# Feed-forward seam of a two-layer decoder trunk: earlier weight loads, sums of squares at other products

## The chip, the cores and the metric

The kernel runs on one core of a Trainium2 chip. The metric is the device time of one execution in microseconds (us). The core has a matrix engine (TensorE, "PE" in the profile), three elementwise engines (VectorE "DVE", ScalarE "ACT", GpSimd "POOL") and a queue engine (SyncE, "SP") that issues nearly all DMA transfers. Each engine executes its own instructions in order, and they wait for each other through semaphores.

## The reference, cut to what matters

A trunk of two layers on one sequence of 1024 tokens with 1024 channels. Layer 0 mixes tokens with a gated recurrent block, layer 1 with attention; each mixer is followed by a SwiGLU feed-forward block of width 2816, and each block is preceded by an RMS norm and added to the residual.

```python
def swiglu_ffn(x, w_in, w_out):
    gu = jnp.einsum("bsd,df->bsf", x, w_in)
    h = jax.nn.silu(gu[..., :D_FF]) * gu[..., D_FF:]
    return jnp.einsum("bsf,fd->bsd", h, w_out)
...
for layer in range(DEPTH):
    hn = rms_norm(h, mix_norm[layer])
    if mixer == 0:
        mixed = rg_lru_block(hn, ..., lru_w_in[j], ..., lru_w_out[j], ...)
    else:
        mixed = stick_breaking_attention(hn, attn_w_qkv[j], attn_w_o[j])
    h = h + mixed
    h = h + swiglu_ffn(rms_norm(h, ffn_norm[layer]), ffn_w_in[layer], ffn_w_out[layer])
return rms_norm(h, final_norm)
```

## The kernel before

**Precision.** Every float32 operand of a matrix product is split into a high and a low part, and a product is three matmuls: high by high, high by low, low by high (`mm3`, lines 155 to 157). In the feed-forward input the parts are float16. So the weights are first scaled by a power of two, taken from a bound on their size: the sum of the squares of all the elements.

**The feed-forward input.** It runs in 22 steps, f = 0 to 21; a step computes 128 gate and 128 up columns for all 1024 tokens. A step is done by a seven-product scheme in the manner of Strassen and Winograd: the weights of a step arrive as two tiles, `ra` (gate columns) and `rb` (up columns), VectorE forms sums and differences of their halves (`s12`, `s2`, `s3`, `do_s4`), and seven products of 12 matmuls each go to PSUM, in the order `ORDER` = 0, 1, 2, 3, 4, 6, 5. Below, "product k" is the k-th of a step, from 0. Steps 4 to 19 work in pairs (`PAIRS` holds the even ones); one product of each pair's two steps is replaced by smaller ones (`inner_part`), for which the weights of both steps are needed together (`inner_sums`).

What happens to the weights of a step:

- `weights_in(f)` loads `ra` and `rb` (512 KB each). Up to f = 4 tiles come from a ring of three raw tiles (`load_raw`, line 128), shared with other weights; a load waits until its tile is free. `rb` of f = 3 and 4 goes to two spare tiles of half the size (`loose`, a ring of 11). From f = 5 on a pool of its own serves.
- `Measure` bounds their size: `square` sums the squares of a tile on ScalarE (line 821; two instructions when the tile comes as two halves), `total` adds up the sums on VectorE (line 919), `factors` adds over partitions with a one-column matmul (`over_partitions`, line 251) and derives the power of two with four small VectorE instructions (`power`, lines 244 to 248). Steps of a pair are measured together.
- `a_hi`, `b_hi`, `c_hi`, `d_hi` write the scaled high parts on ScalarE (line 828), `a_lo` to `d_lo` the low parts on VectorE (line 831). Products 0 and 1 use `wa`, products 2 and 4 `wb`, 3 and 6 `wc`, and product 5 `wd`. `wa` is written during the step before, `wb` (`b_lo`) at the start of its own step, `wc` and `wd` within it. Hence the weights of step f+1 (`nw` in the code) must be measured before `nw.a_hi`, while those of step f+2 (`ahead`) are loaded and squared.

**The engines' order.** The feed-forward runs inside `manual_schedule` for PE, ACT, DVE and POOL: the order of instructions on each of them is the order of the program. The queue engine's is left to the framework's scheduler. In the recurrent stage of layer 0 only PE is ordered by hand.

**The seam.** The output projection of the mixer (16 products, o = 0 to 15 in the code) gives the new residual `h`; its float16 parts for the seven products are written by `v_steps` and `v_last`. Step 0's weights are prepared between these products. Step 0 runs its first six products over three quarters of the contraction (54 matmuls), then over the last quarter (18 matmuls, loop over `k` at line 1210), then the seventh product into half 0 of the PSUM tile `ob`. The power of f = 1 is taken through half 1 of the same tile (`m1.factors(half(ob, 1))`). Step 1, with `s_ == 0` in the code, also holds the sums of squares of the residual (`squares`, `stats_mm`, line 1241) and the norm factors (`factors`, line 1253). `late` marks the steps in which `nw.a_hi` and `nw.a_lo` come at products 4 and 5 (steps 1 and 20); elsewhere they come at 2 and 4.

**Planned jobs.** `measure(x, k, nw, ahead)` is called at product k of step x. It enters `square`, `total` and `factors` of a measurement in `plan` under the pair (step, product) at which they are to be issued, and issues those that are due. In layer 0 it also loads parts of the attention's output weights and takes their maxima (`weigh`, line 627, two per step for eight steps), for a bound that layer 1 needs. After the jobs, at the same product, come the gate's instructions (`gate`: a product with the norm factors, Silu on ScalarE, two more products on VectorE) and the operands of the feed-forward's second half (`operands`).

**The recurrent stage.** In layer 0's mixer the stages of `order` (line 582; A and B project, G computes gates, Y multiplies) are issued one after another. Among them `stage_n(i)` loads one of eight row blocks of `lru_w_out` into a raw tile and sums its squares on ScalarE (line 561).

## Time and profile before

| | |
|---|---|
| median of 3 runs | 2109.04 us (2107.64 to 2115.51) |
| profiled execution, its own time | 2109.0 us |
| its span, first to last instruction | 2106.7 us |
| mean granted PE clock | 0.996 |
| recurrent stage with its projections | about 10 to 250 us |
| layer 0, output projection and feed-forward input | about 250 to 740 us |
| layer 1, the same | about 1400 to 1880 us |

The time runs from launch to end; the span is what the profile covers. In a row of a timeline the columns are: start in us, duration in us, engine, source line, operation, tile written and tiles read, shape, count, and in brackets the time that the engine sat idle before the instruction with what ended it. A row of the waits gives engine, tile and line that waited, what it waited for, then the total in us, the number of times, and the longest. Matmuls overlap: the distance of two starts says more than a duration.

### The profile page before, as it was taken

The page shows a single profiled execution, that of the slowest core. Times are in us where ns is not written, and L with a number is a line of the kernel's source. Part 1 is how long each engine was busy: PE and PEld are TensorE (multiplying, and loading weights), DVE is VectorE, ACT ScalarE, POOL GpSimd, SP SyncE. Part 2 cuts the span into 40 slices and gives each one's busy share as a digit, 9 for nine tenths or more (in the row PEclk, how much of TensorE's full clock was granted, in tenths as well). Part 3 has the DMA queues.
Part 4 walks back from the last instruction along what each step waited for, and adds up shares of the span by engine and source line. Part 5 has one row for each costly group of instructions (what it writes and reads, how often), then busy time and mean ns, then how long its engine had stood idle before and what let it go on. Part 6 is the DMA issues. An engine that isn't in the chain of part 4 may idle for free.

```text
span 2106.7 us, 28516 instructions
## 1 busy us (share of the span) xinstructions
PE 2066.1 (98%) x10052; PEld 1410.3 (67%) x10052; DVE 1824.9 (87%) x2789; ACT 1309.3 (62%) x2111; POOL 155.0 (7%) x130
## 2 busy tenths in 40 slices
PE   8999999999999999999999999999899999999998
PEld 7878885454445478888777777777445555558887
DVE  7878877889999888796999999977799999888886
ACT  6667545665656555466788877754665656554456
POOL 1222010000000000000011111202000000000002
PEclk9999999999999999999999999999999999999999
DMA  7221441445554646433888998963154555565452
GB/s 252 87 67 56 143 157 55 143 137 180 181 185 145 222 150 203 138 121 98 157 179 180 179 174 177 239 212 100 57 184 137 171 164 178 181 211 168 127 154 90
DMA packets 450543, 323.35 MB, mean 153 GB/s; under 512 B 166616, under 2 KB 362336, under 8 KB 450400
## 3 DMA queue, kind: packets, MB, share of 16 engines
q1 hardware_dynamic: 450240, 321.28, 53.2%
q8 instruction: 78, 1.28, 0.2%
q14 instruction: 65, 0.53, 0.1%
q10 hardware_dynamic: 160, 0.27, 0.0%
HBM read 193.01 MB, written 82.84 MB: 131 GB/s over the span
## 4 chain that ended last, share of the span: by engine, by line
PE 79%; DVE 13%; ACT 5%; DMA 1%; issue 1%; POOL 0%; SPq 0%; DVEq 0%; ACTq 0%; POOLq 0%
PE p_ps L157 14%; PE p_ps L155 14%; PE p_ps L156 14%; PE qk_ps L155 4%; PE qk_ps L157 4%; PE qk_ps L156 4%; PE av_ps L2076 3%; PE ob_ps L155 3%; PE ob_ps L157 3%; PE ob_ps L156 3%; PE a_ps L156 2%; PE a_ps L157 2%; PE a_ps L155 2%; PE z_ps L1964 2%; PE z_ps L1965 1%
## 5 line engine op out<-in xcount | busy, mean ns | idle before, releaser
L157 PE MATMUL p_ps<-v,wb 128*128 128x512 f16 x352 | 134.2, 381 | 6.8 <-DVE wb L831 6.8
L155 PE MATMUL p_ps<-v,wb 128*128 128x512 f16 x352 | 133.9, 380 | 0.6 <-ACT G L1084 0.6
L156 PE MATMUL p_ps<-v,wc 128*128 128x512 f16 x352 | 134.1, 381 | 0.0
L157 PE MATMUL p_ps<-v,wc 128*128 128x512 f16 x352 | 134.1, 381 | 0.0
L156 PE MATMUL p_ps<-v,wb 128*128 128x512 f16 x352 | 134.0, 381 | 0.0
L155 PE MATMUL p_ps<-v,wc 128*128 128x512 f16 x352 | 134.0, 381 | 0.0
L828 ACT ACTIVATE wb<-sb,fac 128x1024 f16<-128x1024 f32 x44 | 50.5, 1148 | 104.5 <-DVE sb L760 104.5
L155 PE MATMUL qk_ps<-rh,whi 128*128 128x512 f32 x264 | 112.9, 428 | 0.0
L2002 ACT ACTIVATE w<-z_ps,rs 128x512 f32<-128x512 f32 (+2 forms) x168 | 96.9, 580 | 15.4 <-PE z_ps L1965 13.0
L2024 ACT CAST wx<-w 128x512 f16<-128x512 f32 (+1 forms) x140 | 80.1, 572 | 38.5 <-DVE w L2009 20.4
L156 PE MATMUL qk_ps<-rl,whi 128*128 128x512 f32 x264 | 103.5, 392 | 0.0
L157 PE MATMUL qk_ps<-rh,wlo 128*128 128x512 f32 x264 | 103.5, 392 | 0.0
L2009 DVE TENSOR_TENSOR_SCAN w<-w,unit 128x128 f32<-128x128 f32 (+1 forms) x112 | 93.5, 835 | 9.5 <-ACT w L2002 8.3
L232 POOL TENSOR_TENSOR acc<-acc,rbc 128x512 f32<-128x512 f32 x30 | 42.6, 1419 | 764.9 <-ACT rbc L231 727.1
L155 PE MATMUL a_ps<-xh,whi 128*128 128x512 f32 x248 | 97.0, 391 | 0.0
L156 PE MATMUL a_ps<-xl,whi 128*128 128x512 f32 x248 | 96.6, 390 | 0.1
L157 PE MATMUL a_ps<-xh,wlo 128*128 128x512 f32 x248 | 96.6, 389 | 0.0
L821 ACT ACTIVATE junk<-raw 128x1024 bf16<-128x1024 f32 x84 | 88.5, 1053 | 6.1 <-DMA raw<-in_ffn_w_in 6.1
L1332 DVE TENSOR_TENSOR rl<-rl,rh 128x512 fp32r<-128x512 f32 x128 | 83.4, 685 | 4.9 <-ACT rh L1331 4.9
L2025 DVE TENSOR_TENSOR wx<-w,wx 128x512 f16<-128x512 f32 (+1 forms) x140 | 87.3, 624 | 0.2 <-ACT wx L2024 0.2
L155 PE MATMUL p_ps<-v,wa 128*128 128x512 f16 x224 | 85.2, 380 | 0.0
L156 PE MATMUL p_ps<-v,wa 128*128 128x512 f16 x224 | 85.0, 380 | 0.0
(490 smaller groups left out, 6415.7 us busy)
## 6 DMA issues: line engine op xcount, KB each, us to landing
raw<-in_ffn_w_in SPq DMA_DIRECT2D x84, 512.0 KB, 4.2
rl<-pd SPq DMA_DIRECT2D x128, 256.0 KB, 3.1
pd<-U SPq DMA_DIRECT2D x90, 256.0 KB, 2.3
raw<-in_ffn_w_out SPq DMA_DIRECT2D x56, 256.0 KB, 3.3
raw<-in_attn_w_qkv SPq DMA_DIRECT2D x24, 512.0 KB, 4.3
raw<-in_lru_w_out SPq DMA_DIRECT2D x16, 512.0 KB, 3.6
h<-hd SPq DMA_DIRECT2D x32, 256.0 KB, 5.5
hd<-h SPq DMA_DIRECT2D x32, 256.0 KB, 2.2
```

What stands on the lines that cost most here:

```text
L155: nc.tensor.matmul(ps, lhsT=wh, rhs=mh, start=first, stop=False, **kw)
L156: nc.tensor.matmul(ps, lhsT=wh, rhs=ml, start=False, stop=False, **kw)
L157: nc.tensor.matmul(ps, lhsT=wl, rhs=mh, start=False, stop=last, **kw)
L232: (eng or nc.gpsimd).tensor_add(acc[n], acc[n], sq)
L821: nc.scalar.activation(v["junk"][:, 0 : t.shape[-1]], t, AF.Square, accum_out=next(at))
L828: nc.scalar.activation(hi, t, AF.Copy, scale=self.up)
L1332: V.tensor_sub(tl, f32(tl), f32(th))
L2002: nc.scalar.activation(F, ps[:, 0:n], AF.Sigmoid, scale=rs[:, j : j + 1])
L2009: nc.vector.tensor_tensor_scan(rev, rev, unit[:, NB - n :][:, ::-1], 0.0, op0=ALU.mult, op1=ALU.add)
L2024: nc.scalar.copy(wx[:, 0:m, 0], F)
L2025: nc.vector.tensor_sub(wx[:, 0:m, 1], F, wx[:, 0:m, 0])
L2076: nc.tensor.matmul(ps[:, c0:c1].rearrange("p (j c) -> p j c", c=P), lhsT=VV[q][:, hx, kb], rhs=t, start=first and i == 0, stop=last and i ...
```

## The change

It has five parts.

1. Spare tiles. `rb` of f = 1 to 4 (before: 3 and 4) is loaded as two halves into spare tiles.
2. Sooner loads. f = 2 is loaded at product 15 of the output projection (before: after step 0), f = 3 at product 0 of step 1 (before: products 1 and 2), f = 4 at product 4 of step 1 (before: products 0 and 1 of step 2).
3. Sums of squares. f = 2 is measured inside step 0: the power of f = 1 is taken before the last 18 matmuls, f = 2's squares and total follow, and its factors come at product 0 of step 1 (before: squares, total and factors at products 0 to 2 of step 1). f = 3's squares come at products 3 and 4 of step 1 instead of 4 and 5. f = 4 and 5 are squared at products 0, 1, 4 and 5 of step 2 (before 3 to 6). For all pairs the total comes at product 6 of the even step and the factors at product 2 of the odd one (before: products 0 and 1 of the odd one), and `nw.a_hi` at product 3 of the odd step instead of 2. Step 1 is no longer `late`.
4. Maxima. `weigh` takes the maximum at product 1 of the next step instead of product 6 of the step of the load.
5. Recurrent stage. Loading and squaring the rows of `lru_w_out` are separate, at other places of `order`, some of them later.

```diff
+        rows_in = {}
+
+        def load_rows_in(i):
+            rows_in[i] = load_raw(lru_w_out[0][i * P : (i + 1) * P, :].rearrange("p (a b) -> p a b", a=1), (1,))
+
         def stage_n(i):
-            raw = load_raw(lru_w_out[0][i * P : (i + 1) * P, :].rearrange("p (a b) -> p a b", a=1), (1,))
+            raw = rows_in.pop(i)
             nc.scalar.activation(raw, raw, AF.Square, accum_out=wsq[0][:, i : i + 1])
...
-                if 4 <= i < 4 + 2 * ND and i % 2:
-                    stage_n((i - 4) // 2)
+                for do, at in ((stage_n, (7, 8, 12, 13, 17, 18, 22, 23)), (load_rows_in, (5, 7, 11, 12, 15, 17, 20, 22))):
+                    if i in at:
+                        do(at.index(i))
...
-                if f in (3, 4) and x:
+                if 0 < f < 5 and x:
                     raw = loose(v), loose(v)
...
                     elif o == 15:
                         m1.square(0)
+                        nxt = weights_in(2)
+                        m2 = Measure(nxt)
...
             for i in ORDER0[:6]:
                 part(P0[i], w, i, rhs_in[i], range(HK - 1))
+            m1.factors(half(ob, 1))
+            m2.square(0)
+            m2.square(1)
+            m2.total()
             for k, i in enumerate(ORDER0[:6]):
                 part(P0[i], w, i, rhs_in[i], (HK - 1,))
...
                 elif k == 4:
-                    m1.factors(half(ob, 1))
                     nw.a_hi()
...
             nw.do_s4()
-            nxt = weights_in(2)
             nw.c_hi()
...
-                    plan.setdefault((6 + i // 2, 6), []).append(lambda: weigh(i, t))
+                    plan.setdefault((7 + i // 2, 1), []).append(lambda: weigh(i, t))
...
-                if k == 0 and x in (1, NF - 2):
+                if (x, k) == (1, 0):
+                    m, at = m2, ((1, 0),)
+                elif (x, k) == (NF - 2, 0):
                     m, at = Measure(nw), ((x, 0), (x, 1), (x, 1), (x, 2))
                 elif (x, k) == (1, 3):
-                    m, at = Measure(ahead), ((1, 4), (1, 5), (1, 6), (2, 0))
+                    m, at = Measure(ahead), ((1, 3), (1, 4), (1, 5), (2, 0))
...
-                elif k == 3 and x + 2 in PAIRS:
+                elif (x, k) == (2, 0):
+                    m, at = Measure(ahead, early[3]), ((2, 0), (2, 1), (2, 4), (2, 5), (2, 6), (3, 2))
+                elif k == 3 and x + 2 in PAIRS and x > 2:
                     m = Measure(ahead, early[x + 1])
-                    at = ((x, 3), (x, 4), (x, 5), (x, 6), (x + 1, 0), (x + 1, 1))
+                    at = ((x, 3), (x, 4), (x, 5), (x, 6), (x, 6), (x + 1, 2))
...
-                late = kind == "f" and x in (1, NF - 2)
+                late = kind == "f" and x == NF - 2
+                soon = kind == "f" and x + 1 in PAIRS
...
-                        if nw and not late:
+                        if nw and not late and not soon:
                             nw.a_hi()
...
                         if k == 3:
+                            if soon:
+                                nw.a_hi()
                             nw.s12()
...
                     if kind == "f" and x == 1:
-                        if k == 1:
-                            ahead.load_a()
-                        elif k == 2:
-                            ahead.load_b()
-                    elif kind == "f" and x + 2 in PAIRS:
                         if k == 0:
                             ahead.load_a()
-                        elif k == 1:
                             ahead.load_b()
+                        elif k == 4:
+                            early[2] = weights_in(4)
+                    elif kind == "f" and x + 2 in PAIRS:
+                        if k == 0 and x > 2:
+                            ahead.load_a()
+                        elif k == 1 and x > 2:
+                            ahead.load_b()
+                        if k == 0:
+                            early[x + 1] = weights_in(x + 3, False)
                         elif k == 2:
-                            early[x + 1] = weights_in(x + 3, False)
                             early[x + 1].load_a()
```

## The prediction

> **What bounds the kernel now.** I read the page first, then the waits of TensorE (PE) longest first, then the timelines of PE, VectorE (DVE) and ScalarE (ACT) around each long wait.

> ```profile
> span 2106.7 us, 28516 instructions
> ...
> PE 2066.1 (98%) x10052; PEld 1410.3 (67%) x10052; DVE 1824.9 (87%) x2789; ACT 1309.3 (62%) x2111; POOL 155.0 (7%) x130
> ```

> PE is busy 2066.1 of the 2106.7 us span, so about 40 us of gaps are all that a change of order can win, plus the slow matmuls behind the gaps.

> ```profile
> PE n_ps L251 <- DVE part L919: 9.5, 8, 2.4
> PE p_ps L157 <- DVE wb L831: 6.8, 6, 1.8
> PE ob L155 <- DVE sums L244: 4.9, 2, 2.5
> ```

> All three longest rows belong to the measuring of weights (sums of squares, L919; their power, L244) and to splitting them (L831). PE's timeline in layer 0, with the wait before an instruction in brackets, places four stalls A to D at the start of the feed-forward:

> ```profile
> 340.16 0.38 PE L156 MATMUL p_ps<-v,wc 128*128 128x512 f16 x1
> 340.38 0.38 PE L157 MATMUL p_ps<-v,wc 128*128 128x512 f16 x1
> ...
> 347.12 0.38 PE L155 MATMUL ob<-v,wd 128*128 128x512 f16 x1 [2.45 <-DVE sums L244]
> ...
> 348.48 0.63 PE L155 MATMUL ob<-v,wd 128*128 128x512 f16 x1
> 348.91 0.63 PE L156 MATMUL ob<-v,wd 128*128 128x512 f16 x1
> ...
> 351.04 0.63 PE L155 MATMUL p_ps<-v,wa 128*128 128x512 f16 x1
> ...
> 361.75 0.16 PE L251 MATMUL n_ps<-part,one 128*128 128x1 bf16 x1 [2.42 <-DVE part L919]
> ...
> 382.97 0.38 PE L155 MATMUL p_ps<-v,wb 128*128 128x512 f16 x1 [0.30 <-ACT G L1084]
> ...
> 385.35 0.39 PE L157 MATMUL p_ps<-v,wb 128*128 128x512 f16 x1 [1.79 <-DVE wb L831]
> ...
> 407.05 0.16 PE L251 MATMUL n_ps<-part,one 128*128 128x1 bf16 x1 [2.13 <-DVE part L919]
> ```

> A is 347.12, B 361.75, C 382.97 and 385.35, D 407.05. Matmuls normally start 0.22 us apart (340.16, 340.38), but 0.43 apart at 348.48: after A, B and C the clock is halved for some 3.4 us, about eight matmuls, 1.7 us more each. After D no matmul is slow. Layer 1 has the same four, with a halved clock after A alone:

> ```profile
> 1487.61 0.38 PE L155 MATMUL ob<-v,wd 128*128 128x512 f16 x1 [2.44 <-DVE sums L244]
> ...
> 1501.62 0.16 PE L251 MATMUL n_ps<-part,one 128*128 128x1 bf16 x1 [1.80 <-DVE part L919]
> ...
> 1523.55 0.39 PE L157 MATMUL p_ps<-v,wb 128*128 128x512 f16 x1 [1.79 <-DVE wb L831]
> ...
> 1543.56 0.16 PE L251 MATMUL n_ps<-part,one 128*128 128x1 bf16 x1 [2.14 <-DVE part L919]
> ```

> [...]

> **The change part by part.**

> *Stall A.* Before, f=1's power waits on DVE behind three evictions, and PE's product into the same `ob` tile waits for it. Now its over-partitions matmul stands ahead of the last 18 matmuls of step 0, with f=2's squares and total behind it. The rows of ACT and DVE that feed it:

> ```profile
> 341.80 1.04 ACT L821 ACTIVATE junk<-raw 128x1024 bf16<-128x1024 f32 x1
> ...
> 342.83 0.57 ACT L1064 COPY G<-p_ps 128x512 f32<-128x512 f32 x1
> ...
> 375.74 0.62 ACT L821 ACTIVATE junk<-spare 128x512 bf16<-128x512 f32 x1
> ...
> 377.22 1.28 ACT L1104 ACT_TABLE_LOAD   x1
> ```
> ```profile
> 342.96 0.16 DVE L919 TENSOR_REDUCE part<-sums 128x1 bf16<-128x2 f32 x1
> ...
> 344.06 0.75 DVE L831 SCALAR_TENSOR_TENSOR wd<-s,fac,wd 128x512 f16<-128x512 f32 x1 [0.94 <-ACT wd L828]
> ```

> The square of f=1's second half starts at 341.80 (the casts ahead of it are not touched) and takes 1.03 us; as two loose halves it takes 1.48 (375.74 to 377.22). So its total comes at 343.3 and the matmul at 343.5, while PE has finished the earlier products at 340.38 + 0.38 = 340.76: a **new wait of 2.75 us**, again with a halved clock, in place of 2.45. f=2's squares (1.03 + 1.48 = 2.5 us) then push ACT's `d_hi` and DVE's `wd` from 344.06 to 347.0. PE is at half speed until 348.2, finishes the 18 at 349.1, the 12 of `ob` at 351.65: 0.6 late against 351.04, less 0.35 by which the old slow phase reached into step 1: **+0.25** in each layer. A moves, it does not go.

> *Stall B.* f=2's weights wait for a buffer, and ACT waits for them:

> ```profile
> 360.36 1.06 ACT L821 ACTIVATE junk<-raw 128x1024 bf16<-128x1024 f32 x1 [2.34 <-DMA raw<-in_ffn_w_in]
> ```

> Now they are loaded at product 15 of the output projection, into a slot that step 0's own splitting has freed and two spare tiles, and measured before step 1. Its power follows step 1's first product and waits for nothing. DVE, 2.5 us later than before after A, is next to be late: the sums of squares of the residual end about 0.4 (layer 1: 0.25) after PE wants them. Layer 0: −2.42 − 1.7 + 0.4 = **−3.7**; layer 1: −1.80 + 0.25 = **−1.55**.

> *Stall C.* Before, f=2 is split late, and f=3's squares stand ahead of the first Silu's table load:

> ```profile
> 379.70 1.22 DVE L1106 TENSOR_TENSOR G<-ob,G 128x1024 f32<-128x1024 f32 x1 [2.30 <-ACT G L1104]
> ...
> 384.02 1.27 DVE L831 SCALAR_TENSOR_TENSOR wb<-sb,fac,wb 128x1024 f16<-128x1024 f32 x1
> ```

> DVE loses 2.30 us there. Loading f=3 at the first product of step 1 and squaring one product sooner lets the table load run beside DVE's gate; I leave DVE 1.2 of the 2.3, the length of the Silu itself. Step 2 then begins at 373.7, 3.6 sooner by A and B. The Silu ends at 374.1, and from there to the end of `wb` DVE needs 5.5 us, as it did before from 379.70 to 384.02 + 1.27: 379.6, where PE asks at 379.3. The third matmul of that product came 2.4 us late, of which 0.2 stays: layer 0, −2.4 − 1.7 + 0.2 = **−3.9**; layer 1, −2.4 + 0.15 = **−2.25**.

> *Stall D.* The total of f=4 and f=5 stood behind step 3's splits on DVE. It moves to the end of step 2, its factors to product 2 of step 3, and f=4 lands in step 1: nothing is left for PE to wait for, and step 3's `wb` comes within 0.1 of its time. **−2.1** and **−2.05**.

> The two seams: 0.25 − 3.7 − 3.9 − 2.1 = −9.45, and 0.25 − 1.55 − 2.25 − 2.05 = −5.6; together **−15.05**.

> *The pairs, steps 4 to 19.* The total moves ahead of `b_lo`, the power from product 1 to product 2 of the odd step, `a_hi` one product on (ACT has room). Layer 1, DVE, with one row of ACT and one of PE:

> ```profile
> 1649.39 0.75 DVE L831 SCALAR_TENSOR_TENSOR wc<-s,fac,wc 128x512 f16<-128x512 f32 x1 [0.79 <-ACT wc L828]
> ...
> 1652.57 0.15 DVE L244 TENSOR_SCALAR sums<-n_ps 128x1 f32<-128x1 f32 x1
> ...
> 1653.01 0.14 DVE L248 TENSOR_SCALAR fac<-sums 128x1 int32<-128x1 int32 x1
> ...
> 1654.97 0.75 DVE L831 SCALAR_TENSOR_TENSOR wd<-s,fac,wd 128x512 f16<-128x512 f32 x1 [0.69 <-ACT wd L828]
> ...
> 1666.67 1.28 DVE L831 SCALAR_TENSOR_TENSOR wb<-sb,fac,wb 128x1024 f16<-128x1024 f32 x1
> ```
> ```profile
> 1647.59 1.06 ACT L821 ACTIVATE junk<-raw 128x1024 bf16<-128x1024 f32 x1
> ```
> ```profile
> 1668.23 0.38 PE L157 MATMUL p_ps<-v,wb 128*128 128x512 f16 x1
> ```

> The total now waits on DVE for the fourth square, 1647.59 + 1.06 = 1648.65, some 1.3 us, with `b_lo`, `c_lo` and PE's products behind it. The 0.79 and 0.69 that DVE waits anyway take that up. The power (1652.57 to 1653.01, 0.5 with what it keeps from starting) leaves the shadow of the 0.69 and comes after `wd`, from where DVE runs nearly without a gap: `wb`, ended at 1667.95, ends 0.4 later (0.1 is made up on the way), against PE's need at 1668.23. **+0.2** a pair, seven pairs in layer 1 and three in layer 0: **+2.0** (bounds 0 and 0.5 a pair).

> *The maxima of layer 0* (two, 1.2 us, in each of eight steps):

> ```profile
> 478.93 0.16 PE L251 MATMUL n_ps<-part,one 128*128 128x1 bf16 x1 [0.25 <-DVE part L919]
> ```
> ```profile
> 497.20 0.39 PE L157 MATMUL p_ps<-v,wb 128*128 128x512 f16 x1 [0.80 <-DVE wb L831]
> ```

> 0.25 + 0.80 come four times, 4.2 us. Moved behind the splits, the maxima no longer stand directly ahead of `wb`, but in these steps DVE has nothing to spare: the total's 1.3 us and the power take what the move frees. I find stalls of 0.55 and three of 1.1, so **−0.35** (bounds −4.2 and +2).

> *The recurrent stage.* Squares and loads of `lru_w_out` move; DVE, ACT and the queue are not ordered by hand there.

> ```profile
> 152.42 0.49 PE L155 MATMUL g_ps<-rh,whi 128*128 128x512 f32 x1 [2.22 <-ACT rh L512]
> 153.68 0.74 PE L156 MATMUL g_ps<-rl,whi 128*128 128x512 f32 x1 [0.77 <-DVE rl L513]
> ```
> ```profile
> 114.13 1.06 ACT L561 ACTIVATE raw<-raw 128x1024 f32<-128x1024 f32 x1 [1.09 <-DMA raw<-in_lru_w_out]
> ```

> PE's only stall here is 2.22 + 0.77 and a halved clock, 4.7 us. The chain of waits that ends in it passes the square at 114.13: 1.09 of waiting and 1.06 of work. Whether another square takes that place the trace cannot say. Bounds −4.7 and +4.7 (such a stall again); I take **−2**, nearest to the 2.15 us of that row.

> Sum: −15.05 + 2.0 − 0.35 − 2 = −15.4. The profiled execution took 2109.0 us (span 2106.7, 2.3 outside it), as good as the median, 2109.04: **2093.6**.

> **The rivals.** *R1, the waits only move at C and D as at A.* DVE is 2.5 us later after A; if it stays late, `wb` stalls PE at steps 2 and 3. For it: DVE is nearly full in step 2. Against: its wait of 2.30, which is slack. Only B is won, and the small terms: 0.5 − 3.7 − 1.55 − 0.35, with the pairs and the recurrent stage cancelling, is −5.1: 2104. *R2, slower.* The total in DVE's queue at the end of each even step: if the waits of 0.79 and 0.69 do not absorb its 1.3 us, each pair loses 1.3 + 0.5 = 1.8; 15 pairs, 27 us, against −17.4 for the rest: 2119. It decides once DVE reaches `wd` later than ACT has it. Against it: 0.79 + 0.69 is more than 1.3. *R3, the weights land no sooner*, the queue or a slot holding f=2 and f=3: B and part of C stay, 2101. *R4, more:* all of the recurrent stall (−2.7 more), all maxima (−3.9) and no loss in the pairs (−2): 2085.

> **How the numbers follow.** Chances: the forecast 0.60, R1 0.17, R4 0.12, R2 0.06, R3 0.05. Where the halved clock falls differs from stall to stall, which alone moves the forecast by 3 us. The range leaves out R2 and the edge of R4: 2085 to 2104. A measurement here tells about 0.5%, 10.5 us, from no change; below 2098.5 lie R4 and most of the forecast: 0.70. Within 0.5%: 0.25. Slower: 0.05.

> **What would show it.** Right: PE waits near 340.8 for `part` L919 in both layers; no wait on a load of `in_ffn_w_in` at ACT in step 1; no n_ps stall at steps 1 and 3; small `wb` stalls at each even step. Wrong: no wait at A's new place (faster than I say), `wb` stalls of over 1 us in layer 1's pairs (R2), or a stall longer than 2.2 us in the recurrent stage.

## The result and the profile after

| | before | after |
|---|---|---|
| median of 5 runs | 2112.62 us (2107.64 to 2115.51) | 2098.30 us (2096.75 to 2098.69) |
| ratio after to before, 95% interval | | 0.9935 [0.9919, 0.9951] |
| profiled execution, its span | 2109.0, 2106.7 us | 2098.69, 2096.1 us |
| mean granted PE clock | 0.996 | 0.997 |

The kernel became 0.65% faster, and the whole interval lies on that side. The profiled executions differ by 10.3 us, the medians by 14.3 us: the profiled execution of before lies near the lower end of its runs.

The page of after, and its longest PE waits (engine, tile and line, what it waited for; total in us, times, longest):

```profile
span 2096.1 us, 28530 instructions
...
PE 2063.3 (98%) x10052; PEld 1410.0 (67%) x10052; DVE 1823.8 (87%) x2789; ACT 1311.3 (63%) x2119; POOL 148.5 (7%) x130
```
```profile
PE ob L251 <- DVE part L925: 5.5, 2, 2.7
PE p_ps L157 <- DVE wb L837: 4.3, 6, 0.9
...
PE g_ps L155 <- ACT rh L512: 2.0, 1, 2.0
PE p_ps L155 <- ACT G L1092: 1.6, 5, 0.5
PE p_ps L157 <- DVE wa L837: 1.5, 1, 1.5
PE n_ps L251 <- DVE part L925: 1.2, 2, 0.9
```

The lines of the file moved: L919 is L925 now, L831 is L837, L821 is L827, L1084 is L1092. The stall of n_ps fell from 9.5 to 1.2 us and that of `wb` from 6.8 to 4.3; the wait for `ob` was 4.9 and is 5.5 in a new place. PE's timeline shows the places, first layer 0's seam and step 20, then layer 1's seam:

```profile
344.79 0.16 PE L251 MATMUL ob<-part,one 128*128 128x1 bf16 x1 [2.74 <-DVE part L925]
...
353.42 0.39 PE L157 MATMUL p_ps<-v,wa 128*128 128x512 f16 x1 [1.48 <-DVE wa L837]
...
358.88 0.38 PE L155 MATMUL p_ps<-v,wb 128*128 128x512 f16 x1 [0.52 <-ACT G L1092]
...
381.58 0.39 PE L157 MATMUL p_ps<-v,wb 128*128 128x512 f16 x1 [0.47 <-DVE wb L837]
...
712.29 0.16 PE L251 MATMUL n_ps<-part,one 128*128 128x1 bf16 x1 [0.87 <-DVE part L925]
...
1476.98 0.16 PE L251 MATMUL ob<-part,one 128*128 128x1 bf16 x1 [2.74 <-DVE part L925]
1477.01 0.38 PE L155 MATMUL p_ps<-v,wa 128*128 128x512 f16 x1
...
1478.46 0.63 PE L156 MATMUL p_ps<-v,wa 128*128 128x512 f16 x1
1478.88 0.63 PE L157 MATMUL p_ps<-v,wa 128*128 128x512 f16 x1
```

Stall A is still there (2.74 us at the over-partitions matmul, once in each layer). B and D are gone; of C 0.47 us is left. New are 1.48 us for `wa` in layer 0, 0.52 us for `G` behind it, and 0.87 us at step 20.

To see where time went I took PE's matmuls of both traces in their order and subtracted the start times. The line between A and B is drawn behind the wait for `wa`, ahead of the one for `G`. What each stretch adds, after minus before, beside the forecast:

| stretch | forecast, us | measured, us |
|---|---|---|
| up to step 0 of layer 0 (recurrent stage) | −2 | +1.3 |
| layer 0: A and B | 0.25 − 3.7 = −3.45 | +0.3 − 3.6 = −3.3 |
| layer 0: C | −3.9 | −3.5 |
| layer 0: D | −2.1 | −2.3 |
| layer 0: pairs and maxima | 0.6 − 0.35 = +0.25 | −0.1 |
| layer 0: step 20, and on to layer 1's seam | 0 | +0.75 + 0.1 = +0.85 |
| layer 1: A and B | 0.25 − 1.55 = −1.3 | +0.3 − 1.3 = −1.0 |
| layer 1: C and D | −4.3 | −4.1 |
| layer 1: pairs, step 20, the rest | +1.4 | +1.3 |
| sum | −15.4 | −10.8 |

The two seams gave −9.1 and −5.1, against a forecast of −9.45 and −5.6. The sum is off by 4.6 us, 3.3 of them in the recurrent stage. The seam's terms come again, within 0.02 us, in e1 to e4 and e7, which leave that part of the kernel alone (only D in layer 1 varies, −2.05 to −2.3). So they don't hang on one execution.

### The profile page after: what moved, and what is told of

The parts are those of the page before. It is cut to its first block, busy times and chain, and to the rows that moved or that the text cites. A ratio compares the mean times of both kernels' runs of the same rounds, so it can differ in the third digit from the quotient of the medians.

```text
span 2096.1 us, 28530 instructions
## 1 busy us (share of the span) xinstructions
PE 2063.3 (98%) x10052; PEld 1410.0 (67%) x10052; DVE 1823.8 (87%) x2789; ACT 1311.3 (63%) x2119; POOL 148.5 (7%) x130
## 3 DMA queue, kind: packets, MB, share of 16 engines
q8 instruction: 78, 1.28, 0.3%
## 4 chain that ended last, share of the span: by engine, by line
PE 77%; DVE 14%; ACT 5%; issue 2%; DMA 1%; POOL 0%; SPq 0%; DVEq 0%; ACTq 0%; POOLq 0%
PE p_ps L157 14%; PE p_ps L155 14%; PE p_ps L156 14%; PE qk_ps L155 4%; PE qk_ps L156 4%; PE qk_ps L157 4%; PE av_ps L2094 3%; PE ob_ps L155 3%; PE ob_ps L157 3%; PE ob_ps L156 3%; PE a_ps L156 2%; PE a_ps L157 2%; PE a_ps L155 2%; PE z_ps L1982 2%; PE z_ps L1983 2%
## 5 line engine op out<-in xcount | busy, mean ns | idle before, releaser
L157 PE MATMUL p_ps<-v,wb 128*128 128x512 f16 x352 | 133.8, 380 | 4.3 <-DVE wb L837 4.3
L155 PE MATMUL p_ps<-v,wb 128*128 128x512 f16 x352 | 133.7, 380 | 1.7 <-ACT G L1092 1.6
L156 PE MATMUL p_ps<-v,wb 128*128 128x512 f16 x352 | 133.7, 380 | 0.0
L157 PE MATMUL p_ps<-v,wc 128*128 128x512 f16 x352 | 133.4, 379 | 0.0
L156 PE MATMUL p_ps<-v,wc 128*128 128x512 f16 x352 | 133.4, 379 | 0.0
L155 PE MATMUL p_ps<-v,wc 128*128 128x512 f16 x352 | 133.3, 379 | 0.0
L155 PE MATMUL qk_ps<-rh,whi 128*128 128x512 f32 x264 | 112.9, 428 | 0.0
L156 PE MATMUL qk_ps<-rl,whi 128*128 128x512 f32 x264 | 103.6, 392 | 0.0
L157 PE MATMUL qk_ps<-rh,wlo 128*128 128x512 f32 x264 | 103.5, 392 | 0.0
L155 PE MATMUL a_ps<-xh,whi 128*128 128x512 f32 x248 | 97.1, 391 | 0.0
L156 PE MATMUL a_ps<-xl,whi 128*128 128x512 f32 x248 | 96.6, 390 | 0.1
L157 PE MATMUL a_ps<-xh,wlo 128*128 128x512 f32 x248 | 96.6, 389 | 0.0
L157 PE MATMUL p_ps<-v,wa 128*128 128x512 f16 x224 | 85.4, 381 | 1.5 <-DVE wa L837 1.5
L827 ACT ACTIVATE junk<-raw 128x1024 bf16<-128x1024 f32 x80 | 84.3, 1053 | 3.5 <-DMA raw<-in_ffn_w_in 3.4
L156 PE MATMUL p_ps<-v,wa 128*128 128x512 f16 x224 | 85.3, 381 | 0.0
```

The costliest lines, as they stand in the source:

```text
L155: nc.tensor.matmul(ps, lhsT=wh, rhs=mh, start=first, stop=False, **kw)
L156: nc.tensor.matmul(ps, lhsT=wh, rhs=ml, start=False, stop=False, **kw)
L157: nc.tensor.matmul(ps, lhsT=wl, rhs=mh, start=False, stop=last, **kw)
L827: nc.scalar.activation(v["junk"][:, 0 : t.shape[-1]], t, AF.Square, accum_out=next(at))
```

## The experiments

Each kernel is the kernel after with the edit shown. Two theories stood against each other after the result. **Theory 1**: the seam carries the whole gain; its stalls have moved to what the sums of squares in step 0 hold up, and the stalls at `wb` in layer 0 come from the total that waits on DVE. The rival gives a share of the gain to the other parts, or finds that removing such a wait only brings another. Ratios are to runs of before made beside them, with a median of 2112.11 us for e1 to e4 and 2113.64 us for e5 to e9.

### e1: the seam alone

```diff
-                for do, at in ((stage_n, (7, 8, 12, 13, 17, 18, 22, 23)), (load_rows_in, (5, 7, 11, 12, 15, 17, 20, 22))):
-                    if i in at:
-                        do(at.index(i))
+                if 4 <= i < 4 + 2 * ND and i % 2:
+                    load_rows_in((i - 4) // 2)
+                    stage_n((i - 4) // 2)
...
-                    plan.setdefault((7 + i // 2, 1), []).append(lambda: weigh(i, t))
+                    plan.setdefault((6 + i // 2, 6), []).append(lambda: weigh(i, t))
...
-                    at = ((x, 3), (x, 4), (x, 5), (x, 6), (x, 6), (x + 1, 2))
+                    at = ((x, 3), (x, 4), (x, 5), (x, 6), (x + 1, 0), (x + 1, 1))
...
-                        if nw and not late and not soon:
+                        if nw and not late and not (soon and x == 3):
...
-                            if soon:
+                            if soon and x == 3:
```

> The changed kernel with the recurrent stage, the places of total and factors in steps 4 to 19, a_hi there and the maxima as before; only the seam (loads, spare tiles, squares of f = 1 to 5) is changed. Theory 1, the gain is the seam's alone: matching the matmuls of the two traces, the two seams won 9.1 and 5.1 us and all the rest lost about 3.5; so this kernel takes some 2095 to 2098 us, no slower than the changed one, with the maxima's four pairs of stalls (0.25 and 0.80 us) back and the waits of 2.7 us at the start of step 0's last matmuls as in the changed kernel. Theory 2, the other parts carry some of the gain: 2101 us or more.

Measured: 2094.84 us (2093.31 to 2098.09), ratio 0.9921 [0.9907, 0.9934]. The seam alone is no slower than the whole change, whose interval overlaps. By the traces its two seams gave −9.0 and −4.8 us, those of after −9.1 and −5.1. It ends some 2 us sooner for other reasons: 1.1 us up to step 0, where its clock was not halved in the recurrent stage (see the last section), 1.1 at step 20 of the two layers and right behind it, and 0.3 in layer 1's pairs. Parts 4 and 5 and the pairs' new order are worth nothing that can be measured.

### e2: the recurrent stage back

Only the first hunk of e1.

> The changed kernel with loading and squaring of lru_w_out as before. Theory 1, that part moved nothing but chance: the stall of the gates' matmuls in the recurrent stage is 2.2 + 0.8 us instead of 2.0 + 0.7, and the time is within 2 us of the changed kernel, decided by how many windows of halved clock follow the stall (one before, two in the profiled run of the changed kernel, 1.2 us). Theory 2, the new places earn their keep: 2 us slower or more.

Measured: 2097.10 us, ratio 0.9932 [0.9919, 0.9944], the same as after. PE's stall of the recurrent stage was 2.7 + 0.8 us here, 2.02 + 0.69 in after and 2.22 + 0.77 in before. Over all ten profiles it is 2.7 to 3.4 us in the seven with the new order and 3.0 to 3.4 in the three with the old one. No effect of the place of the squares shows there.

### e3: total and factors of the pairs back

Only the third hunk of e1.

> The changed kernel with total and factors of steps 4 to 19 at products 0 and 1 of the odd step again. Theory 1, VectorE's wait for the fourth square ahead of the total (1.3 us a pair) eats what moving the maxima frees: without it the four stalls of 0.6 to 0.94 us at wb and the small ones of 0.15 to 0.24 us in layer 0 vanish, some 3.5 us less than the changed kernel. Theory 2, VectorE is simply full in these steps: the stalls stay within 0.3 us of what they are, and the time with them.

Measured: 2095.49 us, ratio 0.9922 [0.9909, 0.9934]; by the traces, the pairs of layer 0 are 2.0 us shorter than in after (and step 20 0.9, which is another matter; see the next section). The `wb` stalls of layer 0 (3.3 us) went, but four n_ps stalls of 0.6 us came in their place. Half of the expectation holds: the total is the cause, and its old place is no cure.

### e4: the maxima back

Only the second hunk of e1.

> The changed kernel with the maxima at product 6 of the step of their load, as before. In even steps they then run in VectorE's wait for the fourth square, but in odd steps they stand straight ahead of wb again, with the power of two now behind wd as well. Theory 1: four wb stalls of about 1.2 us (0.8 before plus 0.4 of the power), some 1 us slower than the changed kernel. Theory 2, the place of the maxima does not matter since VectorE's work is the same: stalls and time as in the changed kernel within 0.5 us.

Measured: 2097.03 us, ratio 0.993 [0.9918, 0.9943]. The four `wb` stalls grew from 3.3 to 4.7 us in total, as expected. But the pairs did not become 1 us longer: they took the same time as in after, since small waits elsewhere in them shrank by as much.

With e1 and e3 this makes a square (e1 also has the old place of `nw.a_hi`). Layer 0's pairs against before: 0.0 us with total and maxima both back (e1), −2.1 with the maxima alone moved (e3), −0.1 with the total alone moved (e4), −0.1 with both moved (after). So moving the maxima is worth 2 us where the total stays, and nothing where the total waits on DVE.

### e5: the last square and the total of f = 1 sooner

```diff
+            drain(3)
+            m1.square(1)
+            drain(2)
+            m1.total()
             drain(20)
...
-            m1.square(1)
-            m1.total()
```

> The changed kernel with the square of f = 1's second half and its total a few residual parts sooner (between the last parts of the residual, where ScalarE waits for VectorE), f = 2's squares where the change put them. Theory 1, the wait of 2.7 us at the one-column matmul of step 0 comes from the place of that square alone: it goes, but f = 2's squares still hold back the high part of wd on ScalarE, so that PE waits about 1.5 us at the product into ob, or for wa; net 1.5 us a layer and the halved clock of layer 1, 3 to 4.5 us less than the changed kernel. Theory 2, ScalarE or VectorE is full there and the square delays the residual's parts by its own length: PE waits 1.5 us at the last 18 matmuls instead and nothing is won.

Measured: 2096.22 us, ratio 0.9918 [0.9903, 0.9932]. The median is 2.1 us below that of after, less than expected, and the intervals overlap: the times alone show no gain. PE's timeline of this kernel, in layer 0:

```profile
349.72 0.39 PE L155 MATMUL ob<-v,wd 128*128 128x512 f16 x1 [0.92 <-ACT wd L834]
...
350.51 0.39 PE L157 MATMUL ob<-v,wd 128*128 128x512 f16 x1 [0.18 <-DVE wd L837]
...
354.75 0.39 PE L157 MATMUL p_ps<-v,wa 128*128 128x512 f16 x1 [1.48 <-DVE wa L837]
```

The wait of 2.74 us for `part` is gone, in both layers, and so is the halved clock that followed it in layer 1. But 0.92 + 0.18 us came for `wd`, and the 1.48 for `wa` stands in both layers now: f = 2's squares are still ahead of both on ACT. From the start of the seam to the end this execution is 3.9 us shorter than after, within the expectation; it had lost 2.8 us before that, 2.1 of them at the very start, where the input arrives.

### e6: f = 2's squares behind the splits as well

```diff
-            m2.square(0)
-            m2.square(1)
-            m2.total()
...
                 elif k == 4:
                     nw.a_hi()
+                    m2.square(0)
+                    m2.square(1)
                 elif k == 5:
                     nw.a_lo(2)
+                    m2.total()
```

(with e5's edit)

> As e5_square_early, and f = 2's squares and total after the high and low parts of f = 1's wa. Theory 1: the wait of 2.7 us and those for wa and G behind it go but for some 0.6 us at wa: 3.8 us less in each layer and 1.2 us for the halved clock, 2089 to 2091 us. Theory 2, f = 2 is then measured too late for step 1 and stall B comes back (2 us a layer): as e5_square_early or slower.

Measured: 2091.09 us (2086.99 to 2092.11), ratio 0.9891 [0.9874, 0.9908]; the interval lies below that of after. The whole seam of layer 0, by PE's timeline, with DVE's rows for A's power, for `wd` and for f = 2's total under it (no bracket: DVE did not wait):

```profile
343.08 0.17 PE L251 MATMUL ob<-part,one 128*128 128x1 bf16 x1
...
350.78 0.39 PE L157 MATMUL p_ps<-v,wa 128*128 128x512 f16 x1 [0.60 <-DVE wa L837]
...
356.30 0.38 PE L155 MATMUL p_ps<-v,wb 128*128 128x512 f16 x1 [0.58 <-ACT G L1094]
...
379.01 0.39 PE L157 MATMUL p_ps<-v,wb 128*128 128x512 f16 x1 [0.48 <-DVE wb L837]
```
```profile
345.22 0.15 DVE L244 TENSOR_SCALAR sums<-ob 128x1 f32<-128x1 f32 x1
...
345.73 0.74 DVE L837 SCALAR_TENSOR_TENSOR wd<-s,fac,wd 128x512 f16<-128x512 f32 x1
...
351.30 0.15 DVE L925 TENSOR_REDUCE part<-sums 128x1 bf16<-128x3 f32 x1
```

PE does not wait at A here, and `wd` is ready without a wait. By the traces the term A is −3.5 us in each layer in place of +0.3, the 3.8 us that were expected. B, C and D are within 0.1 us of those of after, so f = 2 is not measured too late. In after DVE waited 0.46, 0.26, 1.68 and 0.94 us in the same place:

```profile
344.58 0.16 DVE L925 TENSOR_REDUCE part<-sums 128x1 bf16<-128x3 f32 x1 [0.46 <-ACT junk L827]
344.99 0.16 DVE L244 TENSOR_SCALAR sums<-ob 128x1 f32<-128x1 f32 x1 [0.26 <-PE ob L251]
...
347.27 0.16 DVE L925 TENSOR_REDUCE part<-sums 128x1 bf16<-128x3 f32 x1 [1.68 <-ACT junk L827]
348.36 0.75 DVE L837 SCALAR_TENSOR_TENSOR wd<-s,fac,wd 128x512 f16<-128x512 f32 x1 [0.94 <-ACT wd L834]
```

So the seam after the change was bounded by ACT's queue: five squares (two halves of f = 1, three pieces of f = 2) directly ahead of `wd`.

### e7: the pairs' squares sooner

```diff
-                    at = ((x, 3), (x, 4), (x, 5), (x, 6), (x, 6), (x + 1, 2))
+                    at = ((x, 3), (x, 4), (x, 4), (x, 5), (x, 6), (x + 1, 2))
```

> The changed kernel with the third and fourth square of each pair from step 4 on one product sooner (products 4 and 5), where ScalarE waits some 2 us for VectorE; total and factors stay. Theory 1, the total's wait of 1.37 us is what leaves VectorE without slack in the steps with maxima: the wait goes, the wb stalls of 3.3 us and the ACT ones of 0.6 us in layer 0 shrink to under 1 us in all, 3 to 4 us less than the changed kernel; in layer 1 the 0.18 us a pair behind the power of two stay. Theory 2, the squares then wait for their loads or push wb's high part back: the stalls stay or grow.

Measured: 2092.07 us (2090.86 to 2093.05), ratio 0.9899 [0.9884, 0.9914], the interval again below that of after. DVE, one pair of layer 0, after and then e7:

```profile
468.62 0.16 DVE L925 TENSOR_REDUCE part<-sums 128x1 bf16<-128x4 f32 x1 [1.37 <-ACT junk L827]
468.69 1.27 DVE L837 SCALAR_TENSOR_TENSOR wb<-sb,fac,wb 128x1024 f16<-128x1024 f32 x1
```
```profile
468.32 0.15 DVE L925 TENSOR_REDUCE part<-sums 128x1 bf16<-128x4 f32 x1
468.39 1.28 DVE L837 SCALAR_TENSOR_TENSOR wb<-sb,fac,wb 128x1024 f16<-128x1024 f32 x1
```

With the fourth square a product sooner the total waits for nothing, and PE's `wb` stalls of 0.60, 0.94, 0.94 and 0.85 us (at 488.74, 525.85, 562.97 and 600.09 in after) are all gone; the pairs of layer 0 gain 4.6 us on after. Step 20's stall is missing here too, but not by this edit: without it e6 has only 0.19 us of it, and with it e9 has 0.31. In layer 1's pairs it gains nothing: there the 1.3 us were hidden.

### e9: e6 and e7 together

> e6_both and e7_squares_sooner together. If both first theories hold and their gains are at different places, they add: 11 to 13 us less than the changed kernel, 2085 to 2087 us. If one of the two falls, its gain is missing here too.

Measured: 2084.42 us (2082.66 to 2086.72), ratio 0.9864 [0.9849, 0.9879]: the lowest median, with an interval below that of e7 and overlapping that of e6 by a little. The gains add: after minus e6 is 7.2, minus e7 6.2, minus both 13.9 us. The traces say the same, with A at −3.5 us in each layer as in e6 and layer 0's pairs at −4.5 (e7: −4.7). Its waits at PE, the whole kernel, for the tiles in question:

```profile
PE g_ps L155 <- ACT rh L512: 2.6, 1, 2.6
...
PE p_ps L157 <- DVE wa L837: 1.2, 2, 0.6
PE p_ps L155 <- ACT G L1094: 1.2, 2, 0.6
PE p_ps L157 <- DVE wb L837: 1.0, 2, 0.5
```

What is left of the two seams is 0.6 + 0.6 + 0.5 us in each layer. About 3 us of the profiled difference is the clock, whose mean was 0.999 in this execution and 0.997 in that of after.

## Why the prediction was right, and where it was not

The range of 2085 to 2104 us and the likeliest sign hold: 2098.30 us, 0.65% faster. The forecast of 2093.6 us is 4.7 us too low. Two things about the sum of −15.4 us were chance. It was taken from 2109.0 us, one of the lowest executions of before; from the median of 2112.62 it leads to 2097.2. And 3.4 us of it are the halved clocks behind B and C, which the last section shows to be a matter of chance. By its own steps:

**Stall A moves, it does not go.** Right: a new wait of 2.74 us for `part`, forecast 2.75, f = 2's squares in front of `wd` on ACT, and +0.3 us in each layer for +0.25. In layer 1 it came as forecast, with a halved clock. In layer 0 the clock was not halved, and PE ran instead into `wa`, 1.48 us late, a wait that the forecast does not have: there the size agrees by luck. e1 shows the two exchanged (halved in layer 0 without a wait, 1.5 us for `wa` in layer 1 without halving), with the same +0.3. So DVE's lateness sets this stretch, and the slow matmuls behind A are hidden in it.

**Stall B.** Right, −3.6 in layer 0 for −3.7 and −1.3 in layer 1 for −1.55: nothing waits for f = 2's load in step 1. I had put what is late next, 0.4 us, to the sums of squares of the residual. It is 0.52 us, 0.7 by the starts of the matmuls, for another reason: PE waits for a PSUM tile whose copy to `G` (L1092) stands behind three casts on ACT, and these behind DVE, late since A:

```profile
355.99 1.15 ACT L834 ACTIVATE wb<-sb,fac 128x1024 f16<-128x1024 f32 x1 [6.62 <-DVE sb L766]
357.04 0.71 ACT L834 ACTIVATE wc<-s,fac 128x512 f16<-128x512 f32 x1
357.65 0.71 ACT L834 ACTIVATE wc<-spare,fac 128x512 f16<-128x512 f32 x1
358.27 0.56 ACT L1092 COPY G<-p_ps 128x512 f32<-128x512 f32 x1
```

e6, where A is gone, still has 0.58 us of this wait, so A is not the whole of DVE's lateness.

**Stall C.** Right in mechanism: DVE's idle time ahead of the first gate product fell from 2.30 to 1.28 us, forecast 1.2. What was left at `wb` is 0.47 us, forecast 0.2 and 0.15: −3.5 for −3.9 in layer 0, −1.8 for −2.25 in layer 1.

```profile
375.93 1.22 DVE L1114 TENSOR_TENSOR G<-ob,G 128x1024 f32<-128x1024 f32 x1 [1.28 <-ACT G L1112]
```

**Stall D.** Right: gone, −2.3 in each layer for −2.1 and −2.05.

**The pairs.** The total's wait of 1.37 us (forecast 1.3) is taken up in layer 1, as forecast. `wb` is 0.18 late there at six of the even steps (forecast 0.2, at seven) and stands without a bracket, since a wait this short shows only as a start 0.36 after the one before in place of 0.22:

```profile
1655.81 0.38 PE L156 MATMUL p_ps<-v,wb 128*128 128x512 f16 x1
1656.17 0.39 PE L157 MATMUL p_ps<-v,wb 128*128 128x512 f16 x1
1656.40 0.38 PE L155 MATMUL p_ps<-v,wb 128*128 128x512 f16 x1
```

What I had missed is that a small wait of before for n_ps, some 0.12 us in each odd step, goes: net +0.3 us in layer 1, not +1.4. That the last row of the table agrees (+1.3 for +1.4) is luck. Its rest is 0.5 us at step 20 and 0.6 just before the end, where one subtraction on DVE (`sb`, at 2053.71) took 1.66 us against 0.55 in before and PE waited for `wbl`. Every kernel with the change loses these 0.6 us; the cause was not looked for.

**The maxima.** The forecast gave stalls of 0.55 and three of 1.1; they are 0.60, 0.94, 0.94 and 0.85. With the pairs the forecast was +0.25 and the result −0.1, for the reason given: e3 and e4 show that moving the maxima is worth something only where the total does not wait on DVE, e7 that the stalls come from that wait. It is R2's mechanism. It decides in layer 0, where DVE has nothing to spare, and costs 4.6 us there (e7).

**The recurrent stage.** This step failed. I took −2, less than half of a stall, on the ground that a square stood in its chain. The stall stayed (2.02 + 0.69 us in after for 2.22 + 0.77, and 2.7 + 0.8 with the old order in e2), and what moved is the clock: halved for 6.8 us instead of 3.4, +1.1 us with the stall's 0.3 taken off. With the new order the clock was halved there for two stretches of 3.4 us (after, e3 to e6), for one (e7) or for none (e9); with the old one for one (before, e2) or none (e1). So the order does not settle it; whether it makes a second stretch likelier, three executions of the old order are too few to say.

**Step 20** is a term that I did not have: a stall of 0.87 us in layer 0 and 0.33 in layer 1, which cost 0.75 and 0.5. The measuring of the last weights came with its load, and ACT waited for it, in before and then in after:

```profile
718.01 1.06 ACT L821 ACTIVATE junk<-raw 128x1024 bf16<-128x1024 f32 x1 [1.20 <-DMA raw<-in_ffn_w_in]
```
```profile
710.90 1.06 ACT L827 ACTIVATE junk<-raw 128x1024 bf16<-128x1024 f32 x1 [1.95 <-DMA raw<-in_ffn_w_in]
```

Before had 0.75 us less of this and no stall at PE. This load goes to the ring of three raw tiles (the pool of its own serves only the odd steps of the pairs). It was not issued later: 712.51 in before, 704.64 in after, and PE was 7.9 us sooner as well. It took longer, 5.50 us from its issue to ACT's square in before and 6.26 in after. In layer 0 of the nine kernels with the change, whose code is the same at this step, this time is 5.19 to 6.26 us, and PE's stall is what exceeds 5.39. So the term is the spread of one transfer. Whether the change makes it longer at all, one profile of before cannot say.

Of the rivals, R1 (waits move at C and D) and R3 (weights land no sooner) fell by PE's timeline. R2 is seen in layer 0 alone, at a small part of its price. R4 is not seen: the recurrent stall stayed.

## What to carry to other kernels

When a load is made to land sooner, ask what its first reader stands in front of: here the squares of the next weights, put ahead of a late split on ACT, kept stall A alive, and clearing that queue (e5's and e6's edits) was worth 7 us more. In layer 0's pairs the sum that waited 1.37 us for its last addend held up what was queued behind it on DVE, so issue the addend a product sooner (e7, two numbers changed, 6 us) before moving the sum. A term for a stall whose release the trace does not tie to the edit should be taken as 0, with its bounds in the range.

## What the runs showed of the hardware

```profile
340.62:344.04 3.42, 1.43 (x7) 1.00 0.00 0
344.04:347.45 3.41, 2.66 (x14) 1.00 0.03 7
347.45:350.86 3.41, 3.41 (x17) 1.00 0.00 0
1473.85:1477.26 3.41, 0.67 (x5) 1.00 0.00 0
1477.26:1480.67 3.41, 3.41 (x10) 0.50 0.00 0
1480.67:1484.08 3.41, 3.41 (x17) 1.00 0.00 0
```

The same stall of 2.74 us falls across a grid point in layer 0, where no stretch has more than 1.99 us idle by these rows (1.974 unrounded) and the clock stays; in layer 1 it lies in one stretch, and the next runs at half clock. D's 2.13 us in layer 0 of before fall across a point as well, as 1.4 and 0.7 us idle, and the clock stays. In the profiles of before and after, from 20 to 2020 us, seven stretches at full clock had 2.02 to 2.83 us idle, and each was followed by a halved one; none of the others, with up to 1.974, was. But in e4's recurrent stage the clock was halved after 1.974. After's second halved stretch in the recurrent stage came behind one with the 0.69 us stall in it; the halved stretches of before held no such stall, and none of them was followed by another. The grid's place against the kernel differs from one profile to the next: its point behind the recurrent stall comes 1.35 us after the start of the matmul that waited in before, and 0.29 us in after. This can make part of the spread of one kernel's times: e6 took a span of 2084.9 us at a mean clock of 1.000 and 2088.4 to 2089.9 at 0.997, and the profiled one of these had 6.8 us at half clock in the recurrent stage, some 3 us of the difference. So a halving behind a stall of 2.0 to 2.7 us, such as these, is a matter of chance. It costs up to 1.7 us (behind A in layer 0 of before, eight matmuls 0.43 us apart in place of 0.22), and nothing where a later wait hides it, as at `wa` (+0.3 us with it and without it in after). No stall under 1.9 us that stood alone brought one here: B's 1.80 us in layer 1 of before lie in one stretch, and the clock stays.
